# A decoder block on one Trainium2 core: the down projection's seven products reordered, with shared PSUM banks and fewer GpSimd additions

## The chip, the cores and the metric

The kernel runs on one NeuronCore of a Trainium2 chip. The metric is the device time of one execution in microseconds (us), as a median over runs. A profile of one execution goes with it; its times are in us from the start of its span.

The engines have these names in the profile: PE is TensorE's matmul, PEld its loading of the stationary operand, DVE is VectorE, ACT is ScalarE, POOL is GpSimd, SP is SyncE, which issues the DMAs here. L1442 is line 1442 of the kernel's file.

## What is computed

The reference is a decoder block for 512 tokens of 2048 channels in float32: RMSNorm, one input projection, three token mixers (dilated attention, a convolution module, windowed attention), an output projection with a residual, and then the feed-forward part, which is all that matters here:

```python
h2 = _rms_norm(x, norm2_g[l])
x = x + (jax.nn.silu(h2 @ w_gate[l]) * (h2 @ w_up[l])) @ w_down[l]
```

`w_gate` and `w_up` are 2048 x 5632, `w_down` is 5632 x 2048. "Down" below is the last product, with the residual.

## The kernel before

**Three matmuls for one.** Each float32 operand is split into a high part and a low part that TensorE takes in a faster format. A product of two operands is then three matmuls: high by high, high by low, low by high. Weights come by DMA as raw float32 into buffers named `21a`, `22b`, `sa` and so on, and `split_up_to` makes the parts: ScalarE casts the raw weights twice (`wn` in PSUM, L269, and `wh`, L270) and VectorE subtracts (`wl`, L271). Splits are made two units ahead of their use (`SPLIT_AHEAD`), into three rotating buffers each of `wh` and `wl`.

**Seven products for eight.** Gate and up, and Down, are both computed in Strassen's manner (Winograd's form): the operands are cut into 2 x 2 blocks, and seven products of sums of these blocks replace eight. On the weights' side the sums are `s`, `21`, `11` and so on, made by GpSimd's additions `plus` (L172) in place, in the raw buffers: `s` = 21 + 11, then 21 = 21 + 22, then 11 = 21 + 11, then 11 = 11 + 12. On the other side the sums of the activations (`a1` to `a7`) are made after gate and up and stored in DRAM as `od`; Down reads them back (`load_next`, L1317).

**Down's work.** The 44 tiles of the inner dimension are 22 pairs, cut into `RANGES` of 4, 3, 4, 3, 4, 4 pairs; for each range there is one block for each half `g` of the output channels. That makes twelve blocks, t = 0 to 11; in the trace their weights are named `d0` to `d11`, with A and B for the two units of a product (the first two pairs, then the rest). Blocks 2, 3, 6 and 7 have three pairs, the others four. `Down.product` runs one product: two units, and in each, two PSUM banks (a = 0 and 1, for two tiles of 128 tokens). A block of four pairs has 24 matmuls of 128x512 in a product, a block of three has 18. The four banks `outs` rotate by two, so a product takes the banks that the product two before it has left.

**The order around it.** Within a unit the program issues, in this order: the weight sums that are due (`sums_now`), the evacuations that are due (`run(evacs)`), the next unit (`next_unit`: casts and splits for two units on, and new weight loads), the matmuls, one read of activations, and `run(extras)`, which holds the DMA stores. `later(n, ...)` puts a function n places further in the queue of evacuations or extras; one place is taken per unit. All engines work through their instructions in this order.

**The sums of the output.** The accumulators `y[g, i, k, a]` hold the output, residual included, in SBUF. In `Down.done` each finished product is added to or subtracted from those that need it. Before the change the order of the products is `D_ORDER` = 7, 1, 5, 6, 4, 2, 3, and every product begins its banks afresh. Product 1 is copied to `u` by ScalarE, product 6 is added to `u` by VectorE (L1458), and GpSimd adds or subtracts `u` in four places: product 1 to `y(0,0)`, then 1 + 6 to `y(1,1)`, `y(1,0)` and `y(0,1)` (two tiles each, so eight additions in a block, L1442). VectorE makes the rest from PSUM, with the same line L1442: four additions after product 7, four after 5, and two after each of 4, 2 and 3, beside the two of 6 into `u`.

**The end.** When a half `g` is finished, `turn_back` transposes the accumulators in 32 x 32 blocks on VectorE (L1349) into tiles `z`, and `put` stores one `z` of two tiles with four DMAs (L1359). `z` takes over a raw weight buffer. The first half (g = 1) is finished after block 10 and is turned back during block 11; the other half is turned back at the end of block 11. The last product of block 11 (`tail` in `Down.product`) is split by output: TensorE makes a = 0, then a = 1 in two halves of 256 columns; the last columns are turned by TensorE transposes (`sides`, L1397) and stored by two DMAs (L1419).

Of the kernel before, what the change touches and what calls it, by code (L numbers as in the profile page):

```python
# [17 lines left out]
T = 512  # L18
# [54 lines left out]

D_ORDER = (7, 1, 5, 6, 4, 2, 3)
# [40 lines left out]
def kernel(ctx: ExitStack, tc: tile.TileContext, xT, wi, wo, wgu, wd, cst_in, outT):  # L117
# [20 lines left out]
    def slot(name, dt=F32, cols=T):  # L138
        return sp.tile([P, cols], dt, name=name, tag="s")
# [1026 lines left out]
    class Up:  # L1166
# [43 lines left out]
        def done(self, first, q, banks):  # L1210
            if first and q == 7:
                self.c = {}
            by = self.keep if first else self.add
            for a, b in enumerate(banks):
                if q == 7:
                    by(1, 1, a, b)
                elif q == 1:
                    by(0, 0, a, b)
                elif q == 4:
                    by(1, 0, a, b)  # L1220
                elif q == 6:
# [75 lines left out]


    feed = []
    for key in D_ORDER:  # L1300
        feed += [(key, j) for j in range(*RANGES[0][:2])]
        feed += [n for n in SUMS if n[0] == DOWN[0][0] and n[1] == (key == 7)] if key in (1, 7) else []
    feed += [n for n in SUMS if n[0] != DOWN[0][0]]
    feed += [(q, j) for r in RANGES[1:] for q in D_ORDER for j in range(*r)]

    def load_next(n, limit=99):
        while feed and n and len(acts) < limit:
# [29 lines left out]
                        ops.pop((q, blk.first + j))  # L1337

    pairs_out = {}

    def turn_back(key, lo=0, hi=T):

        g, i, k, a = key
        if (g, i, k) not in pairs_out:
            c = "AB"[len(pairs_out) % 2]
            name = "22" if g == i == 0 else "s"
            pairs_out[g, i, k] = wp.tile([P, 1024], F32, name=f"z{g}{i}{k}", tag=f"raw{final_bufs[c][name]}", bufs=1)
        z = pairs_out[g, i, k].rearrange("p (b a j) -> p a b j", a=2, j=32)[:, a, lo // 32:hi // 32]
        nc.vector.transpose(z, y[key][:, lo:hi].rearrange("p (b j) -> p b j", j=32))  # L1349
        if hi == T:  # L1350
            y.pop(key)
# [10 lines left out]
    class Down:  # L1362


        def __init__(self, t):
            self.t, (self.g, r) = t, DOWN[t]
            self.pairs = range(*RANGES[r])
            self.drops = t % 2 == 1
            self.final = r == len(RANGES) - 1
            self.end = t == len(DOWN) - 1  # L1370
            self.u = []
# [65 lines left out]
        def sum(self, i, k, a):  # L1437
            return self.g, i, k, a

        def add(self, i, k, a, src, eng, op="tensor_add"):  # L1440
            t = y[self.sum(i, k, a)]
            getattr(eng, op)(t, t, src)  # L1442

        def done(self, q, banks):
            by = nc.vector
            for a, b in enumerate(banks):
                if q == 7:
                    self.add(1, 0, a, b, by)
                    self.add(1, 1, a, b, by)
                elif q == 1:  # L1450
                    self.u.append(slot(f"d{self.t}u{a}"))
                    nc.scalar.copy(self.u[a], b)
                    later(a, self.add, 0, 0, a, self.u[a], nc.gpsimd)
                elif q == 5:
                    self.add(0, 1, a, b, by)
                    self.add(1, 1, a, b, by, "tensor_sub")
                elif q == 6:
                    by.tensor_add(self.u[a], self.u[a], b)  # L1458
                elif q == 4:
                    if self.end:  # L1460

                        if a == 0:
                            turn_back(self.sum(1, 1, 0))
                            turn_back(self.sum(1, 1, 1))
                            later(0, put, self.g, 1, 1)
                            later(1, put, self.g, 1, 0)
                        later(0, turn_back, self.sum(1, 0, a))
                    self.add(1, 0, a, b, by)
                elif q == 2 and self.end:

                    t = slot(f"last{a}")
                    nc.scalar.copy(t, b)
                    self.add(0, 0, a, t, nc.gpsimd)
                elif q == 2:
                    self.add(0, 0, a, b, by)
                else:
                    self.add(0, 1, a, b, by)
            if q == 6:
                for n, (i, k) in enumerate(((1, 1), (1, 0), (0, 1))):
                    for a in range(2):  # L1480
                        later(0 if self.end else (0, 3, 7)[n], self.add, i, k, a, self.u[a], nc.gpsimd,
                              "tensor_add" if i == 0 else "tensor_sub")
            if q == 3 and self.final:
                for n, (i, k) in enumerate(((0, 0), (1, 1), (1, 0), (0, 1))):
                    for a in range(2):
                        later(2 * n + a, turn_back, self.sum(i, k, a))
                    later(2 * n + 2, put, self.g, i, k, queue=extras)

    for t in range(len(DOWN)):
        blk = Down(t)  # L1490
        for k, q in enumerate(D_ORDER):
            blk.product(k, q)
    while evacs or extras:
        run(evacs)
# [83 lines left out]
```

## Time and profile before

| | us |
|---|---|
| median of the three runs | 1853.3 |
| lowest and highest run | 1852.31, 1853.53 |
| the profiled execution's own time | 1851.65 |
| its span, from first to last instruction | 1850.0 |
| TensorE busy (matmuls) | 1841.9 |
| VectorE busy | 1431.4 |
| ScalarE busy | 1320.1 |
| GpSimd busy | 1103.2 |

Down begins at about 1421 us of the span. Its groups of matmuls:

```profile
L1432 PE MATMUL out<-wh,a 128*128 128x512 f32 x620 | 241.4, 389 | 1.5 <-DVE y L1442 0.9
L1433 PE MATMUL out<-wl,a 128*128 128x512 f32 x620 | 241.1, 389 | 0.7 <-DVE wl L271 0.7
L1434 PE MATMUL out<-wh,a 128*128 128x512 f32 x620 | 241.0, 389 | 0.0
```

A group's line gives the source line, the engine, the operation, output and inputs by the program's names, the shape and the count; then the busy time in us, the mean of one in ns, and the idle time just before them with what ended it. Matmuls overlap each other in the pipeline, so one lasts longer (389 ns) than the distance between two starts. A line of the timeline starts with the start and the duration in us. A line of the windows view gives, for each stretch, its length, then the busy time and the number of instructions of PE, PEld, DVE, ACT and POOL, the granted TensorE clock, the busy share of the DMA engines and GB/s.

### The profile page before, as it was taken

How to read it: one execution, taken by the hardware profiler on the slowest of the kernel's cores; microseconds unless marked ns; L12 is line 12 of the kernel's file. 1: busy time of each engine (PE TensorE's matmuls, PEld its weight loads, DVE VectorE, ACT ScalarE, POOL GpSimd, SP SyncE). 2: the span in 40 equal slices, each digit the busy share in tenths (PEclk: the TensorE clock that was granted, in tenths of full speed). 3: DMA queues.
4: the chain of work that ended last, by engine and by line, in shares of the span. 5: the costliest groups of instructions: out<-in, count | busy, mean ns of one | idle time of the engine just before them, and what ended most of it. 6: DMA issues, size and time to landing. Idle time of an engine off the chain costs nothing.

```text
span 1850.0 us, 26616 instructions
## 1 busy us (share of the span) xinstructions
PE 1841.9 (100%) x8370; PEld 1528.4 (83%) x8370; DVE 1431.4 (77%) x2052; ACT 1320.1 (71%) x1794; POOL 1103.2 (60%) x850
## 2 busy tenths in 40 slices
PE   9999999999999999999999999999999999999998
PEld 7888888888888888888888888888888887888887
DVE  6778888998689777777777777777777776777777
ACT  6345644553458788888888878888888877877775
POOL 0125533100003467786778867877768979978775
PEclk9999999999999999999999999999999999999999
DMA  7242243343343356676867777677689878776545
GB/s 275 75 149 82 86 133 106 90 127 137 120 148 103 114 151 188 188 215 181 227 183 205 204 190 225 172 206 214 178 253 289 282 209 276 259 234 224 200 132 114
DMA packets 382989, 330.37 MB, mean 179 GB/s; under 512 B 171648, under 2 KB 311552, under 8 KB 382848
## 3 DMA queue, kind: packets, MB, share of 16 engines
q1 hardware_dynamic: 382704, 328.66, 59.9%
q8 instruction: 67, 1.10, 0.2%
q14 instruction: 74, 0.61, 0.1%
q10 hardware_dynamic: 144, 0.01, 0.0%
HBM read 255.56 MB, written 64.63 MB: 173 GB/s over the span
## 4 chain that ended last, share of the span: by engine, by line
PE 99%; DMA 0%; POOL 0%; DVE 0%; issue 0%; SPq 0%; ACT 0%; DVEq 0%; POOLq 0%; ACTq 0%
PE out L1184 15%; PE out L1182 15%; PE out L1185 15%; PE out L1433 7%; PE out L1432 7%; PE out L1434 7%; PE o L310 3%; PE o L309 3%; PE o L308 3%; PE cq L308 2%; PE cq L309 2%; PE cq L310 2%; PE ak L308 1%; PE aq L308 1%; PE av L308 1%; PE aq L310 1%
## 5 line engine op out<-in xcount | busy, mean ns | idle before, releaser
L1182 PE MATMUL out<-wh,h 128*128 128x512 f32 x1232 | 479.4, 389 | 0.0
L1184 PE MATMUL out<-wl,h 128*128 128x512 f32 x1232 | 479.3, 389 | 0.0
L1185 PE MATMUL out<-wh,h 128*128 128x512 f32 x1232 | 479.3, 389 | 0.0
L1182 PEld LDWEIGHTS out<-wh,h 128*128 128x128 f32 x1232 | 231.2, 188 | 48.1
L1185 PEld LDWEIGHTS out<-wh,h 128*128 128x128 f32 x1232 | 231.2, 188 | 48.0
L1184 PEld LDWEIGHTS out<-wl,h 128*128 128x128 f32 x1232 | 231.2, 188 | 48.0
L1432 PE MATMUL out<-wh,a 128*128 128x512 f32 x620 | 241.4, 389 | 1.5 <-DVE y L1442 0.9
L1433 PE MATMUL out<-wl,a 128*128 128x512 f32 x620 | 241.1, 389 | 0.7 <-DVE wl L271 0.7
L1434 PE MATMUL out<-wh,a 128*128 128x512 f32 x620 | 241.0, 389 | 0.0
L275 ACT CAST wh<-w 128x1024 fp32r<-128x1024 f32 (+2 forms) x94 | 96.9, 1032 | 154.1 <-PE o L309 64.5
L253 DVE TENSOR_TENSOR wl<-w,wh 128x1024 fp32r<-128x1024 f32 (+2 forms) x95 | 113.4, 1193 | 41.9 <-ACT wh L275 40.1
L1432 PEld LDWEIGHTS out<-wh,a 128*128 128x128 f32 x620 | 116.7, 188 | 26.5 <-ACT wh L270 2.4
L1433 PEld LDWEIGHTS out<-wl,a 128*128 128x128 f32 x620 | 116.8, 188 | 24.7 <-DVE wl L271 1.0
L1434 PEld LDWEIGHTS out<-wh,a 128*128 128x128 f32 x620 | 116.8, 188 | 24.1
L1442 DVE TENSOR_TENSOR y<-y,out 128x512 f32<-128x512 f32 x164 | 106.0, 682 | 24.8 <-PE out L1434 23.3
L519 DVE SCALAR_TENSOR_TENSOR y<-bu,cst,y 128x511 f32<-128x511 f32 (+14 forms) x120 | 89.8, 748 | 0.7
L308 PE MATMUL o<-mh_c,wh 128*128 128x512 f32 x128 | 51.1, 399 | 0.0
L308 PE MATMUL cq<-hh,wh 128*128 128x512 f32 x128 | 50.5, 395 | 0.0
L310 PE MATMUL o<-mh_c,wl 128*128 128x512 f32 x128 | 50.0, 391 | 0.0
L309 PE MATMUL cq<-hl,wh 128*128 128x512 f32 x128 | 49.9, 390 | 0.0
L309 PE MATMUL o<-ml_c,wh 128*128 128x512 f32 x128 | 49.9, 390 | 0.0
L310 PE MATMUL cq<-hh,wl 128*128 128x512 f32 x128 | 49.9, 390 | 0.0
(2376 smaller groups left out, 4877.3 us busy)
## 6 DMA issues: line engine op xcount, KB each, us to landing
od<-a SPq DMA_DIRECT2D x154, 256.0 KB, 4.7
a<-od SPq DMA_DIRECT2D x154, 256.0 KB, 5.8
w<-in_wi SPq DMA_DIRECT2D x58, 512.0 KB, 3.3
w<-in_wo SPq DMA_DIRECT2D x32, 512.0 KB, 3.3
x<-in_xT SPq DMA_DIRECT2D x16, 256.0 KB, 6.9
xr<-in_xT SPq DMA_DIRECT2D x16, 256.0 KB, 3.6
x2d<-xr SPq DMA_DIRECT2D x16, 256.0 KB, 2.0
z<-x2d SPq DMA_DIRECT2D x64, 64.0 KB, 3.9
```

What stands on the lines that cost most here:

```text
L253: fn(*args)
L275: (nc.vector.tensor_copy if u == 0 else nc.scalar.copy)(hi[:, :n], t[:, :n])
L308: nc.tensor.matmul(out, wh, xh, start=start, stop=False)
L309: nc.tensor.matmul(out, wh, xl, start=False, stop=False)
L310: nc.tensor.matmul(out, wl, xh, start=False, stop=stop)
L1182: nc.tensor.matmul(b, x[:, high], wh[:, s], start=c == f == 0 and q in (7, 1, 5, 2), stop=False, skip_group_check=True)
L1184: nc.tensor.matmul(b, x[:, high], wl[:, s], start=False, stop=False, skip_group_check=True)
L1185: nc.tensor.matmul(b, x[:, low], wh[:, s], start=False, stop=c == f == 1, skip_group_check=True)
L1432: nc.tensor.matmul(b[:, lo:hi], x[:, high], wh[:, s], start=start, stop=False, skip_group_check=True)
L1433: nc.tensor.matmul(b[:, lo:hi], x[:, high], wl[:, s], start=False, stop=False, skip_group_check=True)
L1434: nc.tensor.matmul(b[:, lo:hi], x[:, low], wh[:, s], start=False, stop=last, skip_group_check=True)
L1442: getattr(eng, op)(t, t, src)
```

## The change

Down takes its products in gate and up's order, `ORDER` = 7, 1, 4, 6, 5, 2, 3. Products 7, 1, 5 and 2 begin their banks afresh; 4, 6 and 3 accumulate on the banks of the product two before, so that these banks hold 7 + 4, 1 + 6 and 5 + 3 at the end. Product 7 is first added alone to `y(1,1)`, 1 alone to `y(0,0)` and 5 alone is subtracted from `y(1,1)`. GpSimd keeps two additions in a block: it subtracts 1 + 6, which ScalarE has copied to `u`, from `y(1,1)`; `y(1,0)` and `y(0,1)` get 1 + 6 from VectorE out of PSUM. In the last block product 5 is also added to `y(0,1)` by itself, since the tail's product 3 begins afresh.

The order of the weights' uses (`works`) and the buffers follow: `12` is loaded into the buffer of `s`, and the four buffers are handed on as in gate and up. At the end, the tiles `z` take over other buffers (`BACK`), and the first half's `turn_back` and `put` calls stand four units later than before.

```diff
-            bufs[c]["12"] = bufs[c]["21"]
+            bufs[c]["12"] = bufs[c]["s"]
...
-            ("s", True), ("11", False), ("21", True), ("11", False), ("22", True), ("12", True), ("11", True)) for c in "AB")
+            ("s", True), ("11", False), ("22", True), ("11", False), ("21", True), ("12", True), ("11", True)) for c in "AB")
...
-        bufs = {c: {"21": b["s"], "s": b["21"], "11": b["22"], "22": b["11"]} for c, b in bufs.items()}
+        bufs = {c: {"21": b["22"], "11": b["21"], "s": b["s"], "22": b["11"]} for c, b in bufs.items()}
...
-    for key in D_ORDER:
+    for key in ORDER:
...
-    feed += [(q, j) for r in RANGES[1:] for q in D_ORDER for j in range(*r)]
+    feed += [(q, j) for r in RANGES[1:] for q in ORDER for j in range(*r)]
...
+    BACK = {(1, 0, 0): ("22", "A"), (1, 1, 1): ("22", "B"), (1, 1, 0): ("21", "A"), (1, 0, 1): ("21", "B"),
+            (0, 1, 0): ("s", "A"), (0, 1, 1): ("s", "B"), (0, 0, 0): ("22", "A"), (0, 0, 1): ("22", "B")}
...
-            c = "AB"[len(pairs_out) % 2]
-            name = "22" if g == i == 0 else "s"
+            name, c = BACK[g, i, k]
...
+            fresh = q in (7, 1, 5, 2)
...
-                        self.multiply(q, banks[a], units[c:], a, 0, T, c == 0, c == 1)
+                        self.multiply(q, banks[a], units[c:], a, 0, T, c == 0 and fresh, c == 1)
...
                 if q == 7:
-                    self.add(1, 0, a, b, by)
-                    self.add(1, 1, a, b, by)
+                    self.add(1, 1, a, b)
                 elif q == 1:
-                    self.u.append(slot(f"d{self.t}u{a}"))
-                    nc.scalar.copy(self.u[a], b)
-                    later(a, self.add, 0, 0, a, self.u[a], nc.gpsimd)
+                    self.add(0, 0, a, b)
+                elif q == 4:
+                    self.add(1, 0, a, b)
+                elif q == 6:
+                    u = slot(f"d{self.t}u{a}")
+                    nc.scalar.copy(u, b)
+                    later(a, self.less, 1, 1, a, u, nc.gpsimd)
+                    self.less(1, 0, a, b)
+                    self.add(0, 1, a, b)
                 elif q == 5:
-                    self.add(0, 1, a, b, by)
-                    self.add(1, 1, a, b, by, "tensor_sub")
-                elif q == 6:
-                    by.tensor_add(self.u[a], self.u[a], b)
-                elif q == 4:
+                    self.less(1, 1, a, b)
                     if self.end:
-
-                        if a == 0:
-                            turn_back(self.sum(1, 1, 0))
-                            turn_back(self.sum(1, 1, 1))
-                            later(0, put, self.g, 1, 1)
-                            later(1, put, self.g, 1, 0)
-                        later(0, turn_back, self.sum(1, 0, a))
-                    self.add(1, 0, a, b, by)
+                        self.add(0, 1, a, b)
...
-                elif q == 2:
-                    self.add(0, 0, a, b, by)
                 else:
-                    self.add(0, 1, a, b, by)
-            if q == 6:
-                for n, (i, k) in enumerate(((1, 1), (1, 0), (0, 1))):
-                    for a in range(2):
-                        later(0 if self.end else (0, 3, 7)[n], self.add, i, k, a, self.u[a], nc.gpsimd,
-                              "tensor_add" if i == 0 else "tensor_sub")
+                    self.add(0, q - 2, a, b)
+            if self.end and q in (6, 5):
+                for a in range(2):
+                    later(a, turn_back, self.sum(1, int(q == 5), a))
+                later(2, put, self.g, 1, int(q == 5))
             if q == 3 and self.final:
                 for n, (i, k) in enumerate(((0, 0), (1, 1), (1, 0), (0, 1))):
                     for a in range(2):
-                        later(2 * n + a, turn_back, self.sum(i, k, a))
-                    later(2 * n + 2, put, self.g, i, k, queue=extras)
+                        later(4 + 2 * n + a, turn_back, self.sum(i, k, a))
+                    later(2 * n + 6, put, self.g, i, k, queue=extras)
```

`less` is `add` with `tensor_sub`.

More of the change, by code (lines that the diff above doesn't have):

```diff
@@ L72 @@
 NBLOCKS = NP // 2
-D_ORDER = (7, 1, 5, 6, 4, 2, 3)
 RANGES = ((0, 4), (4, 7), (7, 11), (11, 14), (14, 18), (18, 22))
@@ L1370, in __init__ @@
             self.end = t == len(DOWN) - 1
-            self.u = []
         def product(self, k, q):
@@ L1438, in sum, with add, less @@
             return self.g, i, k, a
-        def add(self, i, k, a, src, eng, op="tensor_add"):
+        def add(self, i, k, a, src, eng=nc.vector, op="tensor_add"):
             t = y[self.sum(i, k, a)]
             getattr(eng, op)(t, t, src)
+        def less(self, i, k, a, src, eng=nc.vector):
+            self.add(i, k, a, src, eng, "tensor_sub")
         def done(self, q, banks):
-            by = nc.vector
             for a, b in enumerate(banks):
                 if q == 7:
-                    self.add(1, 0, a, b, by)
-                    self.add(1, 1, a, b, by)
+                    self.add(1, 1, a, b)
                 elif q == 1:
-                    self.u.append(slot(f"d{self.t}u{a}"))
-                    nc.scalar.copy(self.u[a], b)
-                    later(a, self.add, 0, 0, a, self.u[a], nc.gpsimd)
-                elif q == 5:
-                    self.add(0, 1, a, b, by)
-                    self.add(1, 1, a, b, by, "tensor_sub")
-                elif q == 6:
-                    by.tensor_add(self.u[a], self.u[a], b)
-                elif q == 4:
-                    if self.end:
-                        if a == 0:
-                            turn_back(self.sum(1, 1, 0))
-                            turn_back(self.sum(1, 1, 1))
-                            later(0, put, self.g, 1, 1)
-                            later(1, put, self.g, 1, 0)
-                        later(0, turn_back, self.sum(1, 0, a))
-                    self.add(1, 0, a, b, by)
+                    self.add(0, 0, a, b)
[7 more added lines that the diff above has]
+                    self.add(0, 1, a, b)
+                elif q == 5:
+                    self.less(1, 1, a, b)
+                    if self.end:
+                        self.add(0, 1, a, b)
                 elif q == 2 and self.end:
@@ L1485, in done @@
                     for a in range(2):
-                        later(2 * n + a, turn_back, self.sum(i, k, a))
-                    later(2 * n + 2, put, self.g, i, k, queue=extras)
+                        later(4 + 2 * n + a, turn_back, self.sum(i, k, a))
+                    later(2 * n + 6, put, self.g, i, k, queue=extras)
     for t in range(len(DOWN)):
         blk = Down(t)
-        for k, q in enumerate(D_ORDER):
+        for k, q in enumerate(ORDER):
             blk.product(k, q)
```

## The prediction

> **What bounds the kernel now.** I read the page's busy times and chain first, to see which engine sets the end:
>
> ```profile
> span 1850.0 us, 26616 instructions
> PE 1841.9 (100%) x8370; PEld 1528.4 (83%) x8370; DVE 1431.4 (77%) x2052; ACT 1320.1 (71%) x1794; POOL 1103.2 (60%) x850
> PE 99%; DMA 0%; POOL 0%; DVE 0%; issue 0%; SPq 0%; ACT 0%; DVEq 0%; POOLq 0%; ACTq 0%
> ```
>
> TensorE is busy for 1841.9 of 1850.0 us. The change keeps every matmul, so it can gain only where TensorE pauses, and it loses wherever it makes TensorE pause. Next, what TensorE waited for, and four stretches of Down (from 1421 us), with TensorE's matmuls in brackets:
>
> ```profile
> PE out L1432 <- DVE y L1442: 0.9, 1, 0.9
> PE out L1433 <- DVE wl L271: 0.7, 1, 0.7
> PE sides L1397 <- DVE y L1411: 0.7, 1, 0.7
> PE out L1432 <- ACT wh L270: 0.7, 1, 0.7
> ```
>
> ```profile
> 1421.00:1540.00 119.00, 119.00 (x527) 98.54 (x526) 85.89 (x105) 89.02 (x111) 101.60 (x69) 1.00 0.74 238
> 1540.00:1545.00 5.00, 2.79 (x11) 1.51 (x9) 4.32 (x7) 4.95 (x10) 5.00 (x7) 1.00 0.75 241
> 1545.00:1552.00 7.00, 7.00 (x24) 5.56 (x25) 5.42 (x8) 5.60 (x10) 7.00 (x7) 0.76 0.92 295
> 1552.00:1850.00 298.00, 293.26 (x1307) 243.05 (x1305) 218.25 (x262) 220.68 (x254) 242.47 (x148) 1.00 0.65 203
> ```
>
> In steady state a matmul takes 119/527 = 0.226 us. So 1540 to 1545 is 11 matmuls short of 22 (2.5 us), and 1545 to 1552, at a granted clock of 0.76, is 7 short of 31 (1.6 us). **Down holds one pause, worth 4.1 us with its slow clock**; three of the four waits stand in it. The chain of waits says where it comes from (start, us, what):
>
> ```profile
> 1531.55 2.39 POOL w('11', 'd3A')_14799 L172
> 1533.94 2.51 POOL y L1442 x2
> 1536.45 0.71 POOL p20a L1144
> 1537.22 0.74 POOL p20l L1145
> 1538.21 0.52 issue
> 1538.73 1.30 POOL w('11', 'd3B')_14824 L172
> ```
>
> GpSimd was late with the weight sum `11` of block 3 (`d3`, t=3), and 2.51 us of that were the `y` additions which the change drops.
>
> I number a block's products 0 to 6; T0 to T6 are their starts. A product has 6 matmuls a pair: 24 with four pairs (5.44 us), 18 with three (4.08 us). Bank a=0 is complete before the product ends: 1.36 us with four pairs, 0.68 with three.
>
> **The change part by part**
>
> *Fewer GpSimd additions.* Eight per block become two:
>
> ```profile
> L1442 POOL TENSOR_TENSOR y<-y,d2u 128x512 f32<-128x512 f32 x8 | 10.2, 1296 | 1.0 <-DVE d2u L1458 1.0
> L1442 DVE TENSOR_TENSOR y<-y,out 128x512 f32<-128x512 f32 x164 | 106.0, 682 | 24.8 <-PE out L1434 23.3 <-POOL y L1442 0.5
> L271 DVE TENSOR_TENSOR wl<-w('11', 'd6A')_15821,wn 128x1024 fp32r<-128x1024 f32 x3 | 3.7, 1218 | 2.0 <-ACT wn L269 2.0
> 1836.13 1.30 DVE L1349 STREAM_TRANSPOSE z<-y 128x512 f32<-128x512 f32 x2
> ```
>
> That is 72 x 1.30 = 93 us less on GpSimd, all beside TensorE; what it gives is the pause: **-4.1 us**. The eight matmul sums of a product pair in PSUM cost nothing extra: VectorE's additions stay at 16 a block, ScalarE's copies at two. What is late next follows.
>
> *A new wait of VectorE on GpSimd.* Product 3's bank (`q` = 6) now holds 1+6. It is copied by ScalarE to `u`, and GpSimd subtracts `u` from `y(1,1)`: half a=0 after unit 9, half a=1 at unit 10, there behind the next block's sum `s`. Directly behind, VectorE must subtract product 4 (`q` = 5) from the same `y(1,1)`, so it stands until GpSimd is through; queued behind it on VectorE is the split `wl` of product 6's weights, which TensorE needs 0.23 us after T6. The sum `s` in turn overwrites the buffer of `12`, and waits until VectorE has split that. Before, the same stretch of block 2 ran so:
>
> ```profile
> 1514.20 1.22 DVE L271 TENSOR_TENSOR wl<-w('12', 'd2A')_14714,wn 128x1024 fp32r<-128x1024 f32 x1
> 1516.84 1.37 DVE L1442 TENSOR_TENSOR y<-y,out 128x512 f32<-128x512 f32 x2 [0.16 <-PE out L1434]
> 1516.88 2.42 POOL L172 TENSOR_TENSOR w('s', 'd3A')_14883<-w('21', 'd3A')_14739,w('11', 'd3A')_14799 128x1024 f32<-128x1024 f32 x1 [0.56 <-ACT wh L270]
> 1518.12 1.21 DVE L271 TENSOR_TENSOR wl<-w('11', 'd2A')_14483,wn 128x1024 fp32r<-128x1024 f32 x1
> 1527.90 2.41 POOL L172 TENSOR_TENSOR w('21', 'd3A')_14739<-w('21', 'd3A')_14739,w('22', 'd3A')_14893 128x1024 f32<-128x1024 f32 x1 [4.39 <-DMA w('22', 'd3A')_14893<-in_wd]
> 1539.98 1.42 POOL L1116 TENSOR_TENSOR a<-p20r,a 128x256 fp32r<-128x256 f32 x2
> 1543.85 0.73 POOL L1149 TENSOR_TENSOR p20r<-p20a,p20r 128x256 f32<-128x256 f32 x1
> 1837.73 0.59 ACT L1472 COPY last<-out 128x512 f32<-128x512 f32 x1 [0.25 <-PE out L1434]
> ```
>
> There product 4's a=0 bank was free at 1516.8, so T5 was 1517.5, and the split (1518.12 to 1519.33) was 2.5 us early for T6 = 1521.6. Now for a block of three pairs, counted from T4: ScalarE's copy (0.59, as the copy at 1837.73) starts at -0.68, so VectorE's four additions (0.62 each in a run) go from 0.0 to 2.5; the split of `12` to 3.7; `s` (2.42) from 3.8 to 6.2; GpSimd's subtraction (1.30) to 7.5; VectorE's (0.68) to 8.2; the split (1.21) to 9.4. TensorE needs it at 2 x 4.08 + 0.23 = 8.4. **So 1.0 us is lost in each three-pair block: 2, 6 and 7.** With four pairs the bank is free 1.36 early and two products take 10.9: there is over 2 us to spare, and I count nothing.
>
> Block 3 has three pairs and pieces of pair 20 on GpSimd too. From the landing of `22` at 1527.9 its queue holds four sums of 2.4 (`21`, `11` twice, `s`), three of 1.3 (the B halves), three of 0.8 and one of 0.73 on p20, six of 0.71 on `a`, and two of 1.30 on `y`: 23.5 us, to 1551.4. VectorE's subtraction and split end at 1553.3. Block 3 starts at 1525.7, so by the matmuls alone TensorE wants the split at 1525.7 + 6 x 4.08 + 0.23 = 1550.4 and the lack is 2.9; 1.0 of it is already spent in block 2's pause, which moves T6 and not the landing: **1.9 us**. Together **+4.9**. The lower bound is 0 (the trace has no such VectorE wait over 0.5 us in all, as the `<-POOL y` of the row above says), the upper is twice, 9. I take the worked value, since each duration is a row's.
>
> *Order and buffers.* Weight sums and loads keep their places in a block; `12` now loads into the buffer of `s`, about three units earlier, and product 2 needs `22` alone, without a sum. Loads, ScalarE's casts and SP's queue in mid-block thus lie where gate and up have them, and the list above names no wait of gate and up's matmuls (L1182 to L1185): 0. If the loads of `12` held SP back, the reads of `a` behind them have a product or more in hand.
>
> *The end.* Two things. Turning back the finished half g=1 is moved four units later (units 5 to 12 of the last block), onto the same products where the other half's transposes now stand; and its last `put` gets place 12 in a queue that runs at units 0 to 11 only, so its four DMAs are issued after everything else.
>
> ```profile
> 1837.35 1.18 DVE L271 TENSOR_TENSOR wl<-w('11', 'd11B')_17406,wn 128x1024 fp32r<-128x1024 f32 x1
> 1839.09 0.59 ACT L1472 COPY last<-out 128x512 f32<-128x512 f32 x1 [0.77 <-PE out L1434]
> 1845.53 0.41 PE L1397 MATMUL sides<-ident,y 128*128 128x128 f32 x2 [0.67 <-DVE y L1411]
> 1841.88 4.85 SPq L1359 DMA_DIRECT2D out_T<-z  x8
> 1846.82 0.89 SPq L1419 DMA_DIRECT2D out_T<-end  x2
> out_T<-z SPq DMA_DIRECT2D x28, 128.0 KB, 3.0
> ```
>
> Before, T6 was 1839.0 (the copy of product 5's second bank starts at 1839.09), the split of the last weights lay ready at 1838.5, the last issue ended at T6 + 8.7 and the span at T6 + 11.0. After, VectorE from T4: four additions behind ScalarE's copies end at 2.0; split, two transposes, split, two transposes (1.2 + 1.3 + 1.2 + 1.3) to 7.0, which is T5 + 1.5; four additions (product 5 now adds to two sums) 2.5, split 1.2 (T5 + 5.2, just in time), two transposes 1.3, split 1.2: T5 + 7.7. TensorE needs this one at T5 + 5.44 + 1.36 + 0.23 = 7.0: 0.7 lost. Two transposes more, T6 + 3.5: only now can the `put` of (0,1,1) start. Behind it SP issues two more puts, the two `end` DMAs and the moved put: 16 issues at 0.55 to 0.6 and 0.9, to about T6 + 13.7, 5.0 later than before; the last put's DMA takes about 3.0 to land, where before the whole span closed 2.3 after the last issue's end. **+5.3**, TensorE's 0.7 (and another 0.7 at its transposes of the tail, which wait for VectorE at T6 + 5.5) inside it. The lower bound is the four issues and a longer landing alone, 2.7; the upper 7.
>
> **The sum:** -4.1 + 4.9 + 5.3 = +6.1 us. The profiled run took 1851.65 us in all (1850.0 and 1.65 around it): 1857.8. The runs' median, 1853.3, is 1.65 above the profiled run, which gives 1859.4; I forecast 1859.
>
> **The rivals**
>
> *Half clock on top.* At 1545 to 1552 the granted clock fell after pauses of 2.5 us within 5, and cost 1.6. Block 3's pause, and the two of the tail, could do it again: 1859 + 2 to 5, some 1862. Against: pauses of 1.0 standing alone are under half of that. The Trainium skill ("TensorE: Matmul & The Clock Gate", Part 1) has the clock halve after about one idle window of 3.4 us and come back after a busy one. By that rule no pause forecast here is long enough, and the time would stay 1859; the row speaks against reading it so strictly, as its pauses were broken by matmuls.
>
> *The new wait is hidden.* If the sums `s` run earlier than worked out (GpSimd is idle there now), blocks 2, 6 and 7 lose nothing and block 3 little: -4.1 + 0 to 1 + 3 to 5.3, so 1853 to 1856, say 1855. For it: the slack is missed by only 1.0. Against: `s` must wait for VectorE's split of `12`, whatever GpSimd has done.
>
> *Faster.* The GpSimd backlog pause may be larger in the timed runs than in the profiled one: their median is 1.65 higher. If that too is this pause, 5.8 us go; with no new wait and only the tail's lower bound of 2.7, the time is 1850. It decides from the point where pauses removed exceed those added by 3.7; that needs both new costs at their lowest.
>
> **How the numbers follow.** Forecast 1859: 0.52; half clock (1862): 0.16; hidden wait (1855): 0.24; faster (1850): 0.08. A measurement of this kernel tells about 0.2%, 3.7 us, from no change: slower means above 1857.0, faster below 1849.6. Slower takes the forecast nearly whole and the half clock: 0.66. Same takes the hidden wait and the forecast's low edge: 0.27. Faster: 0.07. The range reaches from the hidden wait's low end to the half clock: 1853 to 1864.
>
> **What would show it.** Right: no TensorE wait at `d3`'s product 3; waits of TensorE for `wl` at product 6 of blocks 2, 3, 6 and 7, near 1 us, with VectorE idle before a `y` subtraction "<-POOL y"; GpSimd with 26 `y` additions instead of 98; four `out_T<-z` issues after the `end` issues, and T6 to the end of the span 16 us instead of 11. Wrong: TensorE without waits in three-pair blocks, a tail under 13 us, or a pause in the four-pair blocks, which I count free. If gate and up's part before 1421 us moves, something that I did not look at has changed.

## The result, and the profile after

| | before | after |
|---|---|---|
| median of six runs, us | 1852.74 | 1860.77 |
| lowest and highest, us | 1849.86, 1853.53 | 1859.0, 1861.14 |
| profiled execution, us (span) | 1851.65 (1850.0) | 1860.95 (1859.2) |

The ratio is 1.0044 (95% interval 1.0031 to 1.0057): slower by some 8 us. Forecast were 1859, within 1853 to 1864.

The page of the changed kernel first: span, busy times, the chain's shares and the group of VectorE's additions.

```profile
span 1859.2 us, 26562 instructions
PE 1842.0 (99%) x8370; PEld 1526.1 (82%) x8370; DVE 1434.4 (77%) x2054; ACT 1320.6 (71%) x1794; POOL 1013.9 (55%) x778
PE 95%; DVE 1%; POOL 1%; ACT 1%; issue 1%; DMA 1%; SPq 0%; DVEq 0%; ACTq 0%; POOLq 0%
L1442 DVE TENSOR_TENSOR y<-y,out 128x512 f32<-128x512 f32 x190 | 126.4, 684 | 65.6 <-PE out L1434 39.0
```

TensorE works as long as before (1842.0 against 1841.9) and GpSimd 89 us less, yet the span is 9.2 longer: all of it is time in which TensorE stands. The waits view says for what (TensorE's, then VectorE's; the splits are L270 now, since the changed file has one line fewer above them):

```profile
PE out L1433 <- DVE wl L270: 5.3, 6, 1.4
PE sides L1397 <- DVE y L1411: 0.7, 1, 0.7
PE out L1183 <- DVE wl L270: 0.5, 1, 0.5
```

```profile
DVE y L1442 <- POOL y L1442: 15.5, 8, 2.7
```

There are six waits for a split in Down (the third row, 0.5 us, lies ahead of it, in gate and up at 1410), and VectorE stood 15.5 us before `y` additions that GpSimd held up. Block 2 shows the two views' common cause. VectorE, GpSimd and TensorE there (start, us):

```profile
1515.45 2.48 DVE L1442 TENSOR_TENSOR y<-y,out 128x512 f32<-128x512 f32 x4 [0.77 <-ACT d2u L1457]
1517.85 1.21 DVE L270 TENSOR_TENSOR wl<-w('12', 'd2A')_14619,wn 128x1024 fp32r<-128x1024 f32 x1
...
1522.96 0.69 DVE L1442 TENSOR_TENSOR y<-y,out 128x512 f32<-128x512 f32 x1 [2.71 <-PE out L1434]
1523.56 1.22 DVE L270 TENSOR_TENSOR wl<-w('11', 'd2A')_14469,wn 128x1024 fp32r<-128x1024 f32 x1
```

```profile
1515.49 1.29 POOL L1442 TENSOR_TENSOR y<-y,d2u 128x512 f32<-128x512 f32 x1 [2.53 <-ACT d2u L1457]
1519.28 2.41 POOL L171 TENSOR_TENSOR w('s', 'd3A')_14868<-w('21', 'd3A')_14704,w('11', 'd3A')_14779 128x1024 f32<-128x1024 f32 x1 [2.49 <-ACT wh L269]
1521.64 1.28 POOL L1442 TENSOR_TENSOR y<-y,d2u 128x512 f32<-128x512 f32 x1
```

```profile
1523.47 0.39 PE L1432 MATMUL out<-wh,a 128*128 128x512 f32 x1
1524.83 0.50 PE L1433 MATMUL out<-wl,a 128*128 128x512 f32 x1 [0.98 <-DVE wl L270]
1525.17 0.40 PE L1434 MATMUL out<-wh,a 128*128 128x512 f32 x1
```

GpSimd subtracts the first half of `u`, stands, makes `s`, and only then subtracts the second half; VectorE goes on when that is done (1522.92), and TensorE gets its split at 1524.8. (The bracket of VectorE's row names TensorE, since that was the latest event of a wait on several; the bank had been ready for long. Here GpSimd's row must be read beside it.) One thing more is in TensorE's rows: the matmul behind the pause is followed by the next after 0.34 us, not 0.23. The split held TensorE up by 1.13 us here (from 1523.47 to 1524.83, less the usual 0.23); with this slow matmul and small delays behind it the block lost 1.3. So a pause costs some 0.13 to 0.17 more than the delay itself.

For all kernels, this table gives by block what the time from its first matmul to the next block's first has above 42 matmuls a pair at 0.2267 us. T0 is the first matmul of Down, T6 the copy of product 5's second bank, as in the prediction. Ratios are against runs of the kernel before taken beside each kernel. A wait ahead of a block's first matmul counts with the block before it. Times in us.

| kernel | median | ratio (95%) | T0 | d0 | d2 | d3 | d6, d7 | other | T6 | T6 to end | span |
|---|---|---|---|---|---|---|---|---|---|---|---|
| before | 1852.7 | | 1420.8 | 0 | 0 | 4.7 | 0 | 0 | 1839.09 | 10.9 | 1850.0 |
| after | 1860.8 | 1.0044 (1.0031–1.0057) | 1421.1 | 1.7 | 1.3 | 1.8 | 1.3 each | 0 | 1842.17 | 17.0 | 1859.2 |
| e1_end | 1856.4 | 1.0020 (1.0010–1.0030) | 1420.4 | 1.4 | 1.3 | 1.8 | 1.3 each | 0 | 1841.10 | 13.3 | 1854.4 |
| e2_order | 1854.3 | 1.0011 (1.0002–1.0020) | 1420.5 | 0 | 0 | 0.1 | 0 | 0 | 1834.24 | 16.9 | 1851.1 |
| e3_both | 1850.1 | 0.9992 (0.9983–1.0001) | 1420.7 | 0 | 0 | 0.4 | 0 | 0 | 1834.68 | 12.3 | 1847.0 |
| e4_vec | 1855.5 | 1.0017 (1.0008–1.0026) | 1420.5 | 1.3 | 0.2 | 0.2 | 0.2 each | 0 | 1836.31 | 17.4 | 1853.7 |
| e5_pool_back | 1861.1 | 1.0052 (1.0040–1.0065) | 1421.0 | 0 | 0.5 | 2.7 | 0.5 each | 0 | 1838.76 | 17.3 | 1856.1 |
| e6_before_fewer | 1874.5 | 1.0121 (1.0107–1.0135) | 1422.1 | 0.7 | 2.2 | 4.4 | 2.2 each | 12.7 | 1860.13 | 11.5 | 1871.7 |
| e7_put_order | 1859.3 | 1.0044 (1.0031–1.0056) | 1420.2 | 1.7 | 1.3 | 1.8 | 1.3 each | 0 | 1841.18 | 17.0 | 1858.2 |
| e8_u_later | 1852.8 | 1.0007 (0.9998–1.0016) | 1420.6 | 0 | 0 | 5.1 | 0 | 1.7 (d4) | 1841.02 | 10.8 | 1851.8 |
| e9_both_act | 1855.7 | 1.0023 (1.0014–1.0032) | 1422.0 | 0 | 0 | 0.2 | 0 | 0 | 1835.78 | 18.6 | 1854.4 |
| e11_leave_out | 1848.2 | 0.9984 (0.9975–0.9993) | 1420.7 | 0.6 | 0 | 0 | 0 | 0 | 1834.93 | 10.8 | 1845.7 |
| e12_turn_now | 1849.5 | 0.9985 (0.9976–0.9994) | 1421.1 | 0.3 | 0 | 0.1 | 0 | 0 | 1835.11 | 11.6 | 1846.7 |

So the 9.2 us between the two spans are: block 3's pause of before -4.7; new pauses +7.4 (1.7 + 1.3 + 1.8 + 1.3 + 1.3); the end +6.1 (10.9 to 17.0); Down starts later by 0.4.

### The profile page after: what moved, and what is told of

The parts are those of the page before. It is cut to its first block, busy times and chain, and to the rows that moved or that the text cites. A ratio compares the mean times of both kernels' runs of the same rounds, so it can differ in the third digit from the quotient of the medians.

```text
span 1859.2 us, 26562 instructions
## 1 busy us (share of the span) xinstructions
PE 1842.0 (99%) x8370; PEld 1526.1 (82%) x8370; DVE 1434.4 (77%) x2054; ACT 1320.6 (71%) x1794; POOL 1013.9 (55%) x778
## 4 chain that ended last, share of the span: by engine, by line
PE 95%; DVE 1%; POOL 1%; ACT 1%; issue 1%; DMA 1%; SPq 0%; DVEq 0%; ACTq 0%; POOLq 0%
PE out L1183 15%; PE out L1181 15%; PE out L1184 15%; PE out L1433 6%; PE out L1434 6%; PE out L1432 6%; PE o L309 3%; PE o L307 3%; PE o L308 3%; PE cq L307 2%; PE cq L308 2%; PE cq L309 2%; PE ak L307 1%; PE aq L307 1%; PE av L307 1%
## 5 line engine op out<-in xcount | busy, mean ns | idle before, releaser
L1442 DVE TENSOR_TENSOR y<-y,out 128x512 f32<-128x512 f32 x190 | 126.4, 684 | 65.6 <-PE out L1434 39.0
```

## The experiments

**Where GpSimd's second subtraction stands (e2_order).** In `done`, for `q == 6`:

```diff
-                    later(a, self.less, 1, 1, a, u, nc.gpsimd)
+                    later(0, self.less, 1, 1, a, u, nc.gpsimd)
```

> The changed kernel with both halves of u subtracted on GpSimd in the same unit, that is, half a=1 ahead of the next block's sum s instead of behind it. Theory (VectorE waits for a subtraction that stands behind s): the pauses at product 6 of d2, d6 and d7 go (3 x 1.1 = 3.4 us) and those of d0 and d3 at least shrink; the VectorE wait for GpSimd, 15.5 us in all, falls under 6; about 1856 us. The end stays at 17 us. Rival (the splits are late because VectorE now has 16 additions in a tighter order, or because of the shared banks themselves): the pauses stay, 1860.5.

1854.3; no pause is left in Down, and VectorE waits for GpSimd ahead of no `y` addition. Block 2 now, GpSimd and then VectorE:

```profile
1513.12 2.56 POOL L1442 TENSOR_TENSOR y<-y,d2u 128x512 f32<-128x512 f32 x2 [2.53 <-ACT d2u L1457]
1516.91 2.40 POOL L171 TENSOR_TENSOR w('s', 'd3A')_14869<-w('21', 'd3A')_14704,w('11', 'd3A')_14779 128x1024 f32<-128x1024 f32 x1 [1.23 <-ACT wh L269]
```

```profile
1517.20 1.28 DVE L1442 TENSOR_TENSOR y<-y,out 128x512 f32<-128x512 f32 x2
1518.40 1.22 DVE L270 TENSOR_TENSOR wl<-w('11', 'd2A')_14469,wn 128x1024 fp32r<-128x1024 f32 x1
```

Both halves fit into the time in which GpSimd would wait for `s` anyway; VectorE subtracts without a gap. The place of one instruction per block is worth some 6.4 us of the trace: the 7.4 of new pauses (table above) less 0.1 that stays and less 0.9 in block 0 that lies ahead of the first of these subtractions (point 3 below); the medians differ by 6.5. The same banks, products and additions cost nothing, which rules out the rival that the shared banks or VectorE's 16 additions are to blame.

**Without GpSimd's part at all (e4_vec).**

```diff
-                    u = slot(f"d{self.t}u{a}")
-                    nc.scalar.copy(u, b)
-                    later(a, self.less, 1, 1, a, u, nc.gpsimd)
+                    self.less(1, 1, a, b)
```

> The changed kernel without u: VectorE subtracts 1+6 from y(1,1) straight from PSUM, as six additions in a row behind product 3 instead of four, and neither ScalarE nor GpSimd touches y outside the tail. Theory (what is lost is the wait between the two engines, not VectorE's work): the five pauses at product 6 go (5.1 us), although VectorE has 24 additions, 16 us, more; d0's pause at product 2 stays, since that one waits for a product of gate and up; the end is 0 to 1.3 longer; about 1856. Rival (VectorE's load in three-pair blocks is what makes the split late): the pauses stay or grow, 1861 to 1864.

1855.5. With two more VectorE additions in each block the pauses of the three-pair blocks fall to 0.2, so it was not VectorE's load:

```profile
1513.82 3.68 DVE L1442 TENSOR_TENSOR y<-y,out 128x512 f32<-128x512 f32 x6 [0.15 <-PE out L1434]
...
1520.33 1.21 DVE L270 TENSOR_TENSOR wl<-w('11', 'd2A')_14465,wn 128x1024 fp32r<-128x1024 f32 x1
```

In block 0 there stay 1.3, at products 2 and 5. The end is 0.4 longer, as forecast: VectorE's backlog holds TensorE up by 0.6 in the tail.

**Four additions back to GpSimd (e5_pool_back).**

```diff
-                    self.less(1, 0, a, b)
-                    self.add(0, 1, a, b)
+                    later(3, self.less, 1, 0, a, u, nc.gpsimd)   # all blocks but the last
+                    later(7, self.add, 0, 1, a, u, nc.gpsimd)
```

> The changed kernel with 1+6 subtracted from y(1,0) and added to y(0,1) by GpSimd out of u again, three and seven units later as before, in all blocks but the last; VectorE loses four additions a block, order and banks stay. Theory (the gain of the change is GpSimd's 93 us, which clears block 3's pause): a pause of 2 to 4 us returns in block 3 ahead of or at product 6, the pauses of d2, d6 and d7 stay near 1 us or grow; 1862 to 1866. Rival (block 3's pause of before went because of the new order of sums and loads, whatever GpSimd does): block 3 as in the changed kernel, 1860 or less, since VectorE has less to do.

Half of it came. Block 3 loses 2.7 instead of 1.8, in the foretold direction. But blocks 2, 6 and 7 went from 1.3 to 0.5, which I had not expected: VectorE's four additions are the first link of the chain that ends in the late split, and without them `12` is split, and `s` made, earlier. The runs spread from 1857.8 to 1863.4, and the median equals that of the changed kernel. The time decides nothing on the gain of the change. The trace says a little: in block 3 GpSimd again works without a break, from 1526.0 to 1551.5, and starts `s` at T4 + 5.3; in the changed kernel it stood just ahead of `s` and started it at T4 + 4.5.

**The end: the transposes two units earlier (e1_end).**

```diff
-                        later(4 + 2 * n + a, turn_back, self.sum(i, k, a))
-                    later(2 * n + 6, put, self.g, i, k, queue=extras)
+                        later(2 + 2 * n + a, turn_back, self.sum(i, k, a))
+                    later(2 * n + 4, put, self.g, i, k, queue=extras)
```

> The changed kernel with the first half's transposes and puts two units earlier (units 3 to 10 of the last block instead of 5 to 12), so that the last of the four puts again finds a unit. Theory (the end's loss is VectorE's backlog ahead of the last product and the put that falls behind everything else): from the start of the last product to the end of the span 11 to 12.5 us instead of 17.1, no out_T<-z issue behind the end issues, TensorE's pauses before that as in the changed kernel; about 1855.5 us, 4.5 to 6 below it. Rival (the end is longer because product 5's two additions stand at two sums, or because the z tiles lie in other buffers, not because of the place of the transposes): 16 to 17 us as before, 1860.

1856.4; T6 to the end 13.3 instead of 17.0, a little more than expected. SP's queue in the changed kernel with VectorE's transposes, and SP's in this one. SP's rows are shown in two windows for each kernel, since one row over both hides a break between them:

```profile
1837.30 5.21 SPq L1359 DMA_DIRECT2D out_T<-z  x8
1844.91 7.61 SPq L1359 DMA_DIRECT2D out_T<-z  x12
1852.62 0.88 SPq L1419 DMA_DIRECT2D out_T<-end  x2
1853.56 2.33 SPq L1359 DMA_DIRECT2D out_T<-z  x4
```

```profile
1843.60 2.47 DVE L1349 STREAM_TRANSPOSE z<-y 128x512 f32<-128x512 f32 x4
```

```profile
1836.23 5.19 SPq L1359 DMA_DIRECT2D out_T<-z  x8
1842.66 8.33 SPq L1359 DMA_DIRECT2D out_T<-z  x12
1851.09 0.90 SPq L1419 DMA_DIRECT2D out_T<-end  x2
```

In the changed kernel SP has issued eight by 1842.5 and then stands until 1844.91, T6 + 2.7, when the second of VectorE's four transposes is done. From there it issues without a break: 18 issues, to T6 + 13.7. In e1_end it goes on at T6 + 1.6 and has 14 left, to T6 + 10.9. Of the 3.7 us, 1.2 are the earlier start, 1.6 the four issues fewer, and 0.9 the shorter time from the last issue to the end (2.4 instead of 3.3). The edit moves transposes and stores together; no run parts the two.

**Is it the place behind the `end` issues (e7_put_order)?** At the top of `if tail:` one line is added:

```diff
+                run(extras)
```

> The changed kernel with the one store that fell behind the end issues put ahead of the last product's own stores; transposes stay where they are. Theory (SP issues without a break from 1837 to 1856 and the place within this chain matters little): the same number of issues, the last one ends at the same time, the closing is that of the end issue, 2.3 instead of 3.3 us; T6 to the end 16 to 17 us, 1860. Rival (it is the place behind the end issues that costs): the end comes 3 us earlier, 1857.5.

```profile
1843.92 10.89 SPq L1359 DMA_DIRECT2D out_T<-z  x16
1854.90 0.89 SPq L1419 DMA_DIRECT2D out_T<-end  x2
```

T6 to the end stays 17.0. SP stands here too, until T6 + 2.7, so the chain without a break is shorter than I had expected; it again has 18 issues. They take 0.9 longer than in the changed kernel, and the end follows the last one 0.9 sooner. The order of the issues is worth nothing; what is left are the late start and their number.

**Both edits (e3_both).**

> Both edits together: the transposes and puts two units earlier, and both halves of u subtracted ahead of s. If the two costs are separate, the time is the changed kernel less both: no pause in Down before the tail, start of the last product at 1834.2 as with the second edit alone, 13.3 us from there to the end as with the first alone, a span of 1847.5 and 1849 us in all, below the kernel before. Rival (the two overlap: without the pauses of TensorE SP and VectorE have less time for the same stores and transposes, so that the tail grows by what the pauses had given): 1852 or more.

1850.1: no pauses, T6 at 1834.68, then 12.3. The two costs are separate. The median is below that of the kernel before, but the interval (0.9983 to 1.0001) touches no change.

**The gain: additions moved from GpSimd to VectorE in the kernel before (e6_before_fewer).**

```diff
-  later(..., self.add, i, k, a, self.u[a], nc.gpsimd, ...)
+  later(..., self.add, i, k, a, self.u[a], nc.vector if n and not self.end else nc.gpsimd, ...)
```

> The kernel before, with four of the eight GpSimd additions of a block (u to y(1,0) and y(0,1)) on VectorE; order, banks and end untouched, the last block untouched. Theory (block 3's pause comes from GpSimd additions ahead of the weight sum 11): the pause at 1540 to 1552 and the low clock behind it go, 4.1 us, unless VectorE is late somewhere, at most 1 us: 1848.5 to 1850. Rival (that pause comes from the order of the products, which puts 11 early, or from the landing of its load): it stays, 1852.7.

Missed by some 25 us, and on another count than either theory's: pauses in every block.

```profile
PE out L1433 <- DVE wl L271: 16.0, 14, 1.8
```

VectorE beside GpSimd in block 0:

```profile
1453.93 5.94 DVE L1442 TENSOR_TENSOR y<-y,d0u 128x512 f32<-128x512 f32 x2
```

```profile
1451.59 2.57 POOL L1442 TENSOR_TENSOR y<-y,d0u 128x512 f32<-128x512 f32 x2
1454.10 2.41 POOL L172 TENSOR_TENSOR w('s', 'd1A')_14234<-w('21', 'd1A')_14052,w('11', 'd1A')_14139 128x1024 f32<-128x1024 f32 x1
1456.92 2.40 POOL L172 TENSOR_TENSOR w('s', 'd1B')_14261<-w('21', 'd1B')_14141,w('11', 'd1B')_14168 128x1024 f32<-128x1024 f32 x1 [0.41 <-DMA w('11', 'd1B')_14168<-in_wd]
```

The two additions take 5.94 us. They end at 1459.87, 0.55 after GpSimd's second sum (1459.32). Where GpSimd is idle, the same addition takes what one from PSUM takes (block 1):

```profile
1496.13 1.29 DVE L1442 TENSOR_TENSOR y<-y,d1u 128x512 f32<-128x512 f32 x2
```

Both operands, `y` and `u`, lie in SBUF here. Of the 44 such additions the 12 during which GpSimd did nothing took 0.68 to 0.69 each; those that met a GpSimd instruction already under way took up to 3.1. The Trainium skill ("SBUF — State Buffer", SBUF: two separate sides) says that VectorE with two SBUF inputs and a GpSimd operation that reads SBUF take a common port in turn, each for a whole instruction, and that the other one blocks; the trace agrees. The additions out of PSUM that the change uses are not held (650 to 689 ns, 190 of them). So this run left block 3's pause (4.4) undecided, and showed instead why the way through PSUM matters.

**Two additions later in GpSimd's queue (e8_u_later).**

```diff
-  later(0 if self.end else (0, 3, 7)[n], self.add, ...
+  later(0 if self.end else (0, 3, 9 if self.t == 2 else 7)[n], self.add, ...
```

> The kernel before, with one edit: in block 2 alone the last two GpSimd additions of u, to y(0,1), stand two units later, that is, behind the sum 11 of d3B instead of ahead of it. GpSimd's work is the same to the last addition. Theory (block 3's pause is these additions ahead of the sum): 11 of d3B ends 2.5 us earlier, the pauses at 1540 to 1545 fall by 2 us or more and the low clock behind them goes: 1848.5 to 1850.5. Rival (that sum waits for something else, the landing of its load or the pieces of pair 20): the pauses stay, 1852.6.

Neither theory's: 1852.8. The sum `11` of `d3B` did come 1.5 earlier, but the pauses only moved (GpSimd, then TensorE's waits):

```profile
1537.22 1.29 POOL L172 TENSOR_TENSOR w('11', 'd3B')_14824<-w('21', 'd3B')_14801,w('11', 'd3B')_14824 128x512 f32<-128x512 f32 x1
...
1554.48 2.35 POOL L172 TENSOR_TENSOR w('s', 'd4A')_15204<-w('21', 'd4A')_15043,w('11', 'd4A')_15115 128x1024 f32<-128x1024 f32 x1
```

```profile
PE out L1432 <- ACT wh L270: 3.7, 2, 3.2
```

GpSimd is busy without a break from 1531.3 to block 4's `s` at 1554.5, and TensorE now stands 3.2 us for that one. Block 4 starts at 1558.9, where it started at 1558.7 before. My theory as put, that the place of the additions makes the pause, falls: their place only sets where it falls. What is left is their amount.

**The amount alone (e11_leave_out).** In the same loop of the kernel before:

```diff
+                    if (self.t, n) in ((2, 2), (3, 0)):
+                        continue
```

> The kernel before, leaving out four GpSimd additions (u to y(0,1) in block 2, u from y(1,1) in block 3, so those parts of the output lack products 1 and 6 of that block); nothing is put on another engine. Theory, mended after the addition's move by two units changed nothing: block 3's pause is set by the amount of GpSimd's work between the landing of 22 at 1527.9 and block 4's sums s, in whatever order. With 5.1 us less of it the pauses at 1540 and the low clock go and none comes at block 4: 1847.5 to 1849. Rival (the amount is not it, but the landing of 22 or the pieces of pair 20): pauses of 2 us or more stay, 1850.5 or more.

1848.2, and block 3 without a pause. GpSimd comes to the sums of `d3B` and `d4A` at

```profile
1536.17 1.30 POOL L172 TENSOR_TENSOR w('11', 'd3B')_14824<-w('21', 'd3B')_14801,w('11', 'd3B')_14824 128x512 f32<-128x512 f32 x1
...
1548.49 2.40 POOL L172 TENSOR_TENSOR w('s', 'd4A')_15200<-w('21', 'd4A')_15043,w('11', 'd4A')_15113 128x1024 f32<-128x1024 f32 x1
```

The last is 6.0 earlier than with the move, and 4.9 earlier than in the kernel before (1553.4), about what four additions take. Before the change, the amount of GpSimd's work bounds this one stretch.

**What is left of the end (e9_both_act, e12_turn_now).** e9_both_act is e3_both with

```diff
-                        put(self.g, 0, 0)
+                        put(self.g, 0, 0, engs=(nc.sync, nc.scalar))
...
-                        put(self.g, 0, 1, 0, TH)
+                        put(self.g, 0, 1, 0, TH, (nc.sync, nc.scalar))
```

> Both edits together, and in the last product the two puts of y(0,0) and y(0,1) issue every second of their DMAs from ScalarE instead of SP, four issues in all; the copies of the last columns stay on ScalarE. Theory (what is left of the end, 12.3 us from T6 against 10.9 before, is SP issuing without a break until 1844.6, with the last columns ready at 1842.3): the end issues follow the copy directly, T6 to the end 10.8 us, 1.5 less, 1848.5 us in all. Rival (the transposes on VectorE or the landing of the z stores set the end): no change, 1850.

```profile
1838.53 3.36 ACTq L1359 DMA_DIRECT2D out_T<-z  x4
```

```profile
1840.90 10.26 SPq L1359 DMA_DIRECT2D out_T<-z  x15
1851.26 0.88 SPq L1419 DMA_DIRECT2D out_T<-end  x2
```

```profile
SPq L1359 <- DMA out_T<-z: 9.7, 1, 9.7
```

T6 to the end 18.6, worse than with SP alone. SP stands from 1831.2 to 1840.90, between two DMAs of one `put`, and goes on 2.4 us after ScalarE's first issue (1838.53). SP's waits (last row) put these 9.7 us down to the landing of a store. ScalarE's first issue and the one SP goes on with signal the same semaphore in the trace, so that store is ScalarE's; this was not tried by itself. The run says nothing on whether SP is the bound. e12_turn_now asks it in another way, with SP alone:

```diff
-                    later(a, turn_back, self.sum(1, int(q == 5), a))
-                later(2, put, self.g, 1, int(q == 5))
+                    later(0 if q == 5 else a, turn_back, self.sum(1, int(q == 5), a))
+                later(0 if q == 5 else 2, put, self.g, 1, int(q == 5))
```

> Both edits together, and product 5's finished sums y(1,1) of the last block are transposed one after the other ahead of the last split, their store right behind, instead of one in each of the next two units and the store one unit later. Theory (what is left of the end, 12.3 us from T6 against 10.9 before, is SP: from T6 + 1.56 it issues 12 stores without a break and only then the two end issues, whose data lies ready at T6 + 7.6): the store of y(1,1) starts at T6 + 0.5, the end issues at T6 + 7.7, the span ends at T6 + 10.8 to 11.2, and no new pause of TensorE appears; 1849 us or less, below the kernel before by 2 to 3. Rival (with ScalarE's issues gone the wrong way, the earlier store only moves the wait to the transposes of y(0,0), which wait for GpSimd): 12 us from T6, 1850.

```profile
1834.70 8.61 SPq L1359 DMA_DIRECT2D out_T<-z  x13
1843.41 0.89 SPq L1419 DMA_DIRECT2D out_T<-end  x2
```

The first of the 13 issues belongs to the store before. The last three stores start at T6 + 0.4, the `end` issues at T6 + 8.3, the end is at T6 + 11.6: 0.7 earlier, where 1.1 to 1.5 were expected, since 12 issues took 7.8 us (0.65 each). SP is still the bound there. With 1849.5 (ratio 0.9985, interval 0.9976 to 0.9994) this version is faster than both kernels: 2.6 below the kernel before and some 11 below the changed one.

## Why the prediction was right, point by point

1. *The bound.* Right: TensorE's busy time is unchanged, and every difference is a pause, the end, or Down's start.
2. *Fewer GpSimd additions, -4.1.* Right in sign and size: -4.7, counted from matmul to matmul. The reason was put too narrowly. I said GpSimd was late with `11` of block 3 because of the additions ahead of it; in e8_u_later another place only moved the pause, and in e11_leave_out a smaller amount removed it.
3. *The new wait, +4.9.* The mechanism was right, shown by e2_order, and the chain in a three-pair block came as worked out: counted from T4 = 1515.3 (T6 = 1523.47 less two products of 4.08), VectorE's additions end at 2.6 (forecast 2.5), the split of `12` at 3.8 (3.7), `s` at 6.4 (6.2), GpSimd's subtraction at 7.6 (7.5), VectorE's at 8.3 (8.2), the split at 9.5 (9.4). Blocks 2, 6 and 7 lost 1.3 instead of 1.0, of which 0.13 to 0.17 is the slow matmul and the delays behind it.

   Block 3 lost 1.8 for 1.9, and that agreement is luck. The forecast had GpSimd's queue full from the landing of `22` at 1527.9 to its subtraction. In the changed kernel (T4 = 1545.18 in block 3):

```profile
1545.83 2.48 DVE L1442 TENSOR_TENSOR y<-y,out 128x512 f32<-128x512 f32 x4 [1.28 <-ACT d3u L1457]
1549.66 2.41 POOL L171 TENSOR_TENSOR w('s', 'd4A')_15183<-w('21', 'd4A')_15000,w('11', 'd4A')_15089 128x1024 f32<-128x1024 f32 x1 [0.64 <-ACT a L1111]
```

   The sum `21`, which takes the landed `22`, began only at 1529.6, and GpSimd stood 0.64 ahead of `s`. So it was not a full queue that set the time; the chain is that of block 2, begun 0.5 later: VectorE's four additions start at T4 + 0.65 instead of T4 + 0.14, behind ScalarE's copy, which has two casts for pair 20 (0.7 us) ahead of it in the trace. What it would be without them was not tried.

   The step that failed outright is "with four pairs ... I count nothing": block 0 lost 1.7. Of this 0.8 is the same wait at product 6, at which GpSimd subtracts the two halves only at 1448.7 and 1452.3: it has worked without a break since 1428.1, pieces of pair 19 and two multiplications of gate and up's `b10c` among its work, which no later block has. The other 0.9 is a split in product 2 behind two transposes of gate and up's `b10c`, and it goes with the time at which block 0's load of `22` lets GpSimd begin: 3.0 us after Down's first matmul in the changed kernel, 2.6 in e1_end (0.6 lost), 2.3 in e12_turn_now (0.3), 1.7 in e2_order and 0.7 in e3_both (nothing). It differs between executions and was not tried by itself.
4. *Order and buffers, 0.* Right within 0.4: Down's start moved by +0.4 in the profiled run, and by -0.5 to +1.4 in the experiments, whose code ahead of Down is the same. The changed kernel's 0.4 has a wait of 0.5 in gate and up beside it that no other execution shows. Within Down, e2_order and e3_both have the new order and buffers and lose 0.1 and 0.4.
5. *The end, +5.3.* Right in kind, too small: +6.1. Issues ended at T6 + 13.7 as forecast, but by two errors that cancel: SP went on at T6 + 2.7, not T6 + 3.5, and had 18 issues from there, not 16. From the last issue to the end took 3.3, not the 2.6 that the sum had left for it; this is the term that was sized too small. TensorE's 0.7 for the split came to some 0.3. The place of the late put behind the `end` issues, on which I laid weight, is not what costs (e7_put_order): it is that VectorE's transposes let SP go on late, with 18 issues to make.
6. *The sum.* +6.1 forecast, +9.2 in the spans, +8.0 between the medians. That 1859 came so near the 1860.8 is in part luck: the 1.65 that I added for the median of before is no cost of the change. In the result the median of before lies 1.1 above its profiled run, and that of the changed kernel 0.2 below its own.
7. *The rivals.* Half clock on top: no. The granted clock was full in the stretch with the longest pause (columns as in the windows view of the prediction):

```profile
1526.00:1559.00 33.00, 31.63 (x139) 25.63 (x138) 25.55 (x33) 26.99 (x40) 25.99 (x21) 1.00 0.85 277
```

   It was full up to the end of TensorE's work too, so the pauses of the tail cost none. By the Trainium skill ("TensorE: Matmul & The Clock Gate", Part 1) an idle window of about 3.4 us halves the clock. Two traces fit that roughly: no pause here passed 1.4, and the 3.2 us of e8_u_later were followed by the slow clock (1.7 lost in block 4). Others speak against a strict reading: the kernel before has three pauses under 0.9 each ahead of its slow stretch, and e6_before_fewer pauses of 0.5 and 1.8 ahead of one, while a lone pause of 2.3 in e5_pool_back had none behind it. What decides there stays open. Hidden wait: no. Faster: no; but with the wait and the end mended the same change is faster (e12_turn_now), since then the gain is left and little else.

## What to carry to other kernels

A result that VectorE takes from GpSimd in mid-queue should stand on GpSimd ahead of whatever itself waits for VectorE: here the place of one subtraction cost 6.4 us, more than the 4.7 that 89 us of removed GpSimd work brought. An engine at 60% over the span can bound one stretch of it; there the amount of its work counts, and moving an instruction within the stretch only moved the pause. At the end, find when the store queue goes on for the last time and count the issues it then has, at 0.6 to 0.7 us each here; a merged row of the timeline can hide the break before them.

## What was not expected of the hardware

- VectorE's addition of two SBUF operands (128x512) took 0.68 us beside an idle GpSimd and up to 3.1 beside its sums; from one SBUF and one PSUM operand it took 0.65 to 0.69 throughout.
- After a pause of TensorE of 0.4 to 1.4 us, at the full granted clock, the first matmul was followed after 0.34 us instead of 0.23.
- ScalarE's four issues in the tail lengthened it by 6.3 us (18.6 against 12.3); SP stood 9.7 us for the landing of a store meanwhile.
